# Folding three banks' maxima ahead of time in an attention loop on one core

## The chip, the core and the metric

The kernel runs on one core of a Trainium2 chip. Five engines matter: TensorE (PE in the profile; its weight loads are PEld), VectorE (DVE), ScalarE (ACT), GpSimd (POOL) and SyncE (SP), which issues the DMAs. Each engine works through its own queue in the order in which the program wrote it; semaphores tie the queues together. TensorE writes its results to PSUM, eight banks of 512 float32 columns in each of 128 partitions; everything else lives in SBUF or in HBM. The metric is the time of one execution in microseconds on the device; lower is better.

## What is computed

One layer of an encoder, for two sequences: a prompt of 512 rows and a sample of 2,048 rows, each 1,024 wide, all in float32. The input projection gives a pooled branch and an attention branch; after the output projection comes a gated feed-forward network with a convolution of width 3. The change touches attention alone:

```python
q_full = concatenate([q_nope, q_rope], -1)      # 8 heads, 64 + 32 wide
k_full = concatenate([k_nope, k_rope of all heads], -1)
s = einsum('bqhd,bkhd->bhqk', q_blk, k_full) * scale
p = softmax(s, axis=-1)
o = einsum('bhqk,bkhd->bqhd', p, v)             # v is 64 wide
```

Products are made from float16 halves: each operand is split into a high and a low part, and three of the four products are added up. That gives nearly float32.

## The kernel before

Attention is cut into 144 units. A unit is one head and one block of queries: 256 queries in the prompt (16 units, `nq` 2), 128 queries in the sample (128 units, `nq` 1). The scores of a unit lie transposed in PSUM: keys on the partitions, and in each bank four tiles of keys by 128 queries (in the prompt two tiles by 256). A sample unit has four banks, a prompt unit two. Seven of the eight PSUM banks rotate through the scores of successive units (`bank`, from psS and psT); the eighth, `x` (psX, `side_tile`), holds the small things of a unit side by side: the output of the products in its first 129 columns, and the transposed maxima in others.

A softmax needs, for each query, the maximum over all keys. With the scores transposed, the maximum runs over the partitions and over the tiles. The steps, with their letters in the written order and their lines, are these for unit `i`:

- scores of a bank on PE: twelve matmuls, L939 (L for bank 3 of unit i+1; a, b, c for banks 0, 1, 2 of unit i+2).
- maximum of a bank over its four tiles, on DVE: a reduction that reads PSUM, L951 (M for bank 3 of unit i+1; x, y, z for banks 0, 1, 2 of unit i+2). Bank `b` writes the adjacent 128 columns `mx4[:, b, :]`.
- fold (N, unit i+1): one DVE reduction over the four banks, L965. It reads `mx4` with its two last axes exchanged, so in steps of 128 values.
- T (unit i+1): the folded maxima are transposed on PE into `x`, L981, so that queries lie on partitions.
- d (unit i+1): DVE reduces them over the 128 columns (L989), which gives the maximum of each query, and splits it into two parts that add up exactly (L992, L995, four columns wide each).
- R (unit i+1): the parts are transposed back by PE (L1003), and ACT copies them out with the sign changed (mr, L1006).
- r (unit i): four small matmuls add the negative maximum to the four banks, L1015, at once in four row groups of the array.
- e0, e1 (unit i): ACT takes the exponential of a bank into `pf` in SBUF as float32, L1028. It frees the bank.
- h, f, i (unit i): the high half of `pf` in float16: bank 0 on ACT (L1042), bank 1 and then banks 2 and 3 together on DVE (L1040).
- l0 to l3 (unit i): the low half, one POOL subtraction for each bank, L1047.
- A, P (unit i-2): sixteen pairs of matmuls multiply the halves with the values, L1062 and L1063, ten pairs in A and six in P.
- o (unit i-2): ACT copies the output out of `x`, L1075, and after each fourth block POOL adds its halves, L1078. q: after each fourth block DVE divides by the sum, L1090 and L1096.

Between units a generator (`prep`) is advanced by one step in two units of four, from unit 36 on: it loads and scales the output projection's weights; 16 of its steps are a DVE reduction, L832.

The order within a unit is written by hand as a string, `ORDER` for units followed by a sample unit and `ORDER2` for the others; `START` has the first five. The framework keeps each engine's instructions in this order (`manual_schedule`) and adds semaphores for data and for buffers.

Of the kernel before, what the change touches and what calls it, by code (L numbers as in the profile page):

```python
# [11 lines left out]
F32 = mybir.dt.float32  # L12
F32R = mybir.dt.float32r
I32 = mybir.dt.int32
AF = mybir.ActivationFunctionType
ALU = mybir.AluOpType
AX = mybir.AxisListType
# [3 lines left out]
P = 128  # L21
# [27 lines left out]
def encoder(ctx, tc, ins, outs, seq_names=("x_prompt", "x_sample")):  # L49
    nc = tc.nc  # L50
    act, dve, pool, pe = nc.scalar, nc.vector, nc.gpsimd, nc.tensor
# [21 lines left out]
    ident = small([P, P], "ident")  # L73
# [140 lines left out]
    with tp("wA", 1) as wA, tp("pA", 2) as pA, tc.manual_schedule():  # L214
# [568 lines left out]
        k = NC - 1  # L783
# [109 lines left out]
    with tp("pB", 2) as pB, tp("psX", 1, "right", space=PSUM) as psX, \  # L893
# [9 lines left out]
        units = []  # L903
# [39 lines left out]
        def st_max(i, b):  # L943
            u = units[i]
            w = u["w"]
            t0, t1 = u["banks"][b]
            st = u["st"][b]
            if t1 - t0 == 4:
                if b == 0:
                    u["mx4"] = pB.tile([P, 4, P], F32, name=f"mx4_{i}", tag="mx4")  # L950
                dve.tensor_reduce(u["mx4"][:, b, :], st.rearrange("p (t q) -> p q t", q=w), axis=AX.X, op=ALU.max)  # L951
            elif b:
                for t in range(2):
                    dve.tensor_tensor(out=u["mx"][:, :w], in0=st[:, t * w:(t + 1) * w], in1=u["mx"][:, :w], op=ALU.max)
            else:
                u["mx"] = pB.tile([P, 256], F32, name=f"mx_{i}", tag="mx")
                dve.tensor_reduce(u["mx"][:, :w], st[:, :(t1 - t0) * w].rearrange("p (t q) -> p q t", q=w), axis=AX.X,
                                  op=ALU.max)

        def st_fold(i):  # L960

            u = units[i]
            if len(u["banks"]) == 4:
                u["mx"] = pB.tile([P, 256], F32, name=f"mx_{i}", tag="mx")
                dve.tensor_reduce(u["mx"][:, 0:P], u["mx4"].rearrange("p b q -> p q b"), axis=AX.X, op=ALU.max)  # L965

        def side_tile(i):

            if ("x", i) not in state:
                state["x", i] = psX.tile([P, 512], F32, name=f"x_{i}", tag="x")  # L970
            return state["x", i]

        def st_T(i):
            u = units[i]
            xp = side_tile(i - 1)
            old = units[i - 1 - LAG]["nq"] if i > LAG else 1
            u["alone"] = u["nq"] > 1 or old > 1
            u["mrp"] = xp[:, 512 - u["w"]:] if u["alone"] else xp[:, 129:129 + P]
            xp = u["xp"] = xp[:, 512 - u["w"]:]
            for j in range(u["nq"]):  # L980
                pe.matmul(xp[:, j * P:(j + 1) * P], u["mx"][:, j * P:(j + 1) * P], ident, is_transpose=True,  # L981
                          start=u["alone"], stop=True, skip_group_check=True)

        def st_redT(i):
            u = units[i]
            nq = u["nq"]
            mc = pB.tile([P, 2], F32, name=f"mc_{i}", tag="mc")
            m = mc[:, 0:nq]
            dve.tensor_reduce(m, u["xp"][:, :nq * P].rearrange("p (j k) -> p j k", j=nq), axis=AX.X, op=ALU.max)  # L989
            hi, lo = p3[:, 0:nq, :, 0], p3[:, 0:nq, :, 1]  # L990
            mb = m.rearrange("p (j o) -> p j o", o=1).to_broadcast([P, nq, 4])
            dve.tensor_scalar(out=hi.bitcast(I32), in0=mb.bitcast(I32), scalar1=-4096, scalar2=None,  # L992
                              op0=ALU.bitwise_and)
            for j in range(nq):
                dve.tensor_scalar(out=lo[:, j], in0=mb[:, j], scalar1=p3[:, j, 0, 0:1], scalar2=None,  # L995
                                  op0=ALU.subtract)

        def st_rep(i):

            u = units[i]  # L1000
            nq, w = u["nq"], u["w"]
            for j in range(nq):
                pe.matmul(u["mrp"][:, j * P:(j + 1) * P], p3[:, j].rearrange("p a b -> p (a b)"), ident,  # L1003
                          is_transpose=True, start=u["alone"], stop=True, skip_group_check=True)
            mr = pB.tile([P, 256], F32R, name=f"mr2_{i}", tag="mr2")
            act.activation(mr[:, :w], u["mrp"][:, :w], AF.Copy, scale=-1.0)  # L1006
            u["mr"] = mr

        def st_r1(i, b):
# [9 lines left out]
        def cols(u, b):  # L1019
            t0, t1 = u["banks"][b]  # L1020
            return slice(t0 * u["w"], t1 * u["w"])
# [9 lines left out]
        def st_hi(i, b):  # L1031
            u = units[i]
            if "ph" not in u:
                u["ph"] = pB.tile([P, 2048], F16, name=f"ph_{i}", tag="ph", bufs=3)
                u["pl"] = pB.tile([P, 2048], F16, name=f"pl_{i}", tag="pl", bufs=3)
            c = cols(u, b)
            if b == 2 and len(u["banks"]) == 4:
                c = slice(c.start, cols(u, 3).stop)
            if b in (1, 2):
                dve.tensor_copy(u["ph"][:, c], u["pf"][:, c])  # L1040
            elif b == 0:
                act.activation(u["ph"][:, c], u["pf"][:, c], AF.Copy)  # L1042

        def st_lo(i, b):
# [70 lines left out]
        def run(fn, k, *a):  # L1115
            if 0 <= k < NU:
                fn(k, *a)

        def some(fn, k, bs):
            if 0 <= k < NU:  # L1120
                for b in bs:
                    if b < len(units[k]["banks"]):
                        fn(k, b)
# [1 line left out]
        step = dict(  # L1125
            r=lambda i: some(st_r1, i, range(4)),
            e=lambda i: some(st_exp, i, range(4)),
            e0=lambda i: some(st_exp, i, range(3)),
            e1=lambda i: some(st_exp, i, [3]),
            A=lambda i: run(st_pv, i - LAG, 0),  # L1130
            P=lambda i: run(st_pv, i - LAG, 1),
            
            L=lambda i: some(st_scores, i + 1, [3]),
            a=lambda i: some(st_scores, i + 2, [0]),
            b=lambda i: some(st_scores, i + 2, [1]),
# [6 lines left out]
            x=lambda i: some(st_max, i + 2, [0]),  # L1142
            y=lambda i: some(st_max, i + 2, [1]),
            z=lambda i: some(st_max, i + 2, [2]),
            N=lambda i: run(st_fold, i + 1),
            f=lambda i: some(st_hi, i, [1]),
            h=lambda i: some(st_hi, i, [0]),
            i=lambda i: some(st_hi, i, [2]),
            l0=lambda i: some(st_lo, i, [0]),
            l1=lambda i: some(st_lo, i, [1]),  # L1150
            l2=lambda i: some(st_lo, i, [2]),
# [5 lines left out]
            q=lambda i: run(st_out2, i - LAG - 1))  # L1157
        START = ["a b x y", "a b T d t x u y R", "r e T d t R x y u f l1 h l0",
                 "r e T d t R x y u f l1 h l0", "r e T d A P R x y f l1 h l0 o q"]
        ORDER2 = "r e T d a b x R f l1 y h A P q o l0 c z"  # L1160
        ORDER = "r e0 A L M N P o e1 a T d f l1 b R i c h l0 l2 l3 x y z q"
        for i in range(-2, NU):
            whole = units[min(max(i, 0) + 1, NU - 1)]["nq"] == 1
            for x in (START[i + 2] if i + 2 < len(START) else ORDER if whole else ORDER2).split():
                step[x](i)
            if i >= NU // 4 and i % 4 in (0, 1):
                next(prep, None)
            if i == NU - 8:
                for _ in prep:
                    pass  # L1170
                c_load_m(0)
                c_load_m(1)
# [549 lines left out]
```

## Time and profile before

| | us |
|---|---|
| median of three runs (3251.7 to 3269.7) | 3259.68 |
| the profiled execution, its own time | 3256.74 |
| its span, from the first to the last instruction | 3254.9 |
| PE busy in the span | 3044.8 |
| DVE busy in the span | 2161.2 |
| attention stage, from the first add of maxima to the last exponential | 359 to 1272 |

The profile is one execution. "Busy" is the time in which an engine has an instruction under way; PE's matmuls overlap, so a busy PE can still be slower than at its peak. A table of waits says which engine stood idle, on which instruction, until what. A timeline lists instructions in order of time and merges those of one kind. The granted clock of TensorE is given as a share of 2.4 GHz; it has two levels, 1.2 and 2.4 GHz.

### The profile page before, as it was taken

The page shows a single profiled execution, that of the slowest core. Times are in us where ns is not written, and L with a number is a line of the kernel's source. Part 1 is how long each engine was busy: PE and PEld are TensorE (multiplying, and loading weights), DVE is VectorE, ACT ScalarE, POOL GpSimd, SP SyncE. Part 2 cuts the span into 40 slices and gives each one's busy share as a digit, 9 for nine tenths or more (in the row PEclk, how much of TensorE's full clock was granted, in tenths as well). Part 3 has the DMA queues.
Part 4 walks back from the last instruction along what each step waited for, and adds up shares of the span by engine and source line. Part 5 has one row for each costly group of instructions (what it writes and reads, how often), then busy time and mean ns, then how long its engine had stood idle before and what let it go on. Part 6 is the DMA issues. An engine that isn't in the chain of part 4 may idle for free. (4 is left out here: it accounts for less than half of the span.)

```text
span 3254.9 us, 59928 instructions
## 1 busy us (share of the span) xinstructions
PE 3044.8 (94%) x24601; PEld 1959.7 (60%) x24601; DVE 2161.2 (66%) x4783; ACT 1400.4 (43%) x2863; POOL 875.7 (27%) x825
## 2 busy tenths in 40 slices
PE   6999888888887888999999999999999999999998
PEld 4777577777776776444555555555545555555554
DVE  6677788788887887335777777734357666674333
ACT  4554556556565665223333333433333333333333
POOL 1211467777776775221000000000100000000000
PEclk9999899999998999999999999999999999999999
DMA  3333221201110102576111111311161111113112
GB/s 133 105 108 92 72 50 34 70 5 24 31 22 8 28 4 75 190 220 168 45 47 40 40 39 40 112 36 36 57 150 40 51 41 39 40 38 102 42 38 75
DMA packets 272061, 210.37 MB, mean 65 GB/s; under 512 B 48739, under 2 KB 247722, under 8 KB 271530
## 3 DMA queue, kind: packets, MB, share of 16 engines
q1 hardware_dynamic: 270012, 200.23, 21.1%
q0 software_dynamic: 1440, 5.24, 0.4%
q8 instruction: 193, 3.16, 0.4%
q10 hardware_dynamic: 334, 1.06, 0.1%
q14 instruction: 82, 0.67, 0.1%
HBM read 140.51 MB, written 55.38 MB: 60 GB/s over the span
## 5 line engine op out<-in xcount | busy, mean ns | idle before, releaser
L1288 PE MATMUL up<-h,ws 128*128 128x512 f16 (+1 forms) x6336 | 1146.6, 344 | 7.3 <-DMA h<-h_x_sample 5.9
L1288 PEld LDWEIGHTS <-ws 128*128 128x128 f16 x6336 | 619.9, 98 | 533.3 <-issue 6.1
L1047 POOL TENSOR_TENSOR pl<-pf,ph 128x512 f16<-128x512 f32 x544 | 660.6, 1242 | 239.9 <-DVE ph L1040 197.0
L1387 PE MATMUL dn<-G,wds 128*128 128x512 f16 (+1 forms) x3168 | 579.0, 344 | 0.0
L939 PE MATMUL st<-Q,K 96*128 96x128 f16 (+1 forms) x6336 | 469.4, 225 | 3.3 <-ACT pf L1028 2.1
L1387 PEld LDWEIGHTS <-wds 128*128 128x128 f16 x3168 | 310.0, 98 | 254.2
L939 PEld LDWEIGHTS <-K 96*128 96x128 f16 x6336 | 420.9, 102 | 14.7 <-issue 3.8
L1028 ACT ACTIVATE pf<-st,ln_shift,cs 128x512 f32<-128x512 f32 x544 | 392.7, 774 | 56.6 <-PE st L1015 47.0
L951 DVE TENSOR_REDUCE mx<-st 128x128 f32<-128x512 f32 x512 | 329.3, 684 | 70.3 <-PE st L939 69.5
L1293 ACT ACTIVATE c<-up,ctab 128x511 f32<-128x511 f32 (+3 forms) x264 | 182.1, 699 | 407.4 <-PE up L1288 401.0
L1294 DVE SCALAR_TENSOR_TENSOR c<-up,ctab,c 128x510 f32<-128x510 f32 (+3 forms) x264 | 173.5, 657 | 185.7 <-ACT c L1293 183.0
L1062 PE MATMUL x<-V,ph 128*128 128x129 f16 x2072 | 238.4, 232 | 0.4 <-ACT t L1075 0.4
L1063 PE MATMUL x<-V,pl 128*128 128x65 f16 x2072 | 228.9, 202 | 6.6 <-POOL pl L1047 6.6
L1062 PEld LDWEIGHTS <-ph 128*128 128x128 f16 x2176 | 211.3, 105 | 32.3 <-issue 32.2
L1063 PEld LDWEIGHTS <-pl 128*128 128x128 f16 x2176 | 207.2, 103 | 7.7 <-POOL pl L1047 7.3
L1394 DVE SCALAR_TENSOR_TENSOR yt<-dn,yscB,yt 128x512 f32<-128x512 f32 (+1 forms) x48 | 31.5, 660 | 227.5 <-ACT yt L1393 217.7
L1297 DVE SCALAR_TENSOR_TENSOR c<-up,ctab,c 128x511 f32<-128x511 f32 (+1 forms) x264 | 174.7, 662 | 9.3
L1006 ACT ACTIVATE mr<-x 128x128 fp32r<-128x128 f32 (+1 forms) x143 | 41.2, 288 | 276.0 <-PE x L1003 276.0
L130 ACT ACTIVATE ws<-wr,sF 128x1024 f16<-128x1024 f32 x88 | 96.2, 1138 | 147.0 <-DVE sF L1265 142.0
L1335 POOL PARTITION_ALL_REDUCE imrA<-imxA x2 | 0.7, 374 | 576.9 <-DVE imxA L1333 576.9
L1262 POOL PARTITION_ALL_REDUCE war<-wam x22 | 7.8, 356 | 527.0 <-DVE wam L1260 520.6
L1415 POOL TENSOR_TENSOR y<-y,fng 128x512 f32<-128x512 f32 (+1 forms) x42 | 45.3, 1083 | 384.4 <-ACT yp L1406 349.7
(410 smaller groups left out, 3716.4 us busy)
## 6 DMA issues: line engine op xcount, KB each, us to landing
wr<-in_w_up SPq DMA_DIRECT2D x88, 512.0 KB, 4.9
wd<-in_w_down SPq DMA_DIRECT2D x32, 512.0 KB, 4.3
x_s<-in_x_sample SPq DMA_DIRECT2D x8, 1024.0 KB
xt_Cs<-in_x_sample SPq DMA_DIRECT2D x8, 1024.0 KB, 7.8
x_x_sample<-xt_Cs SPq DMA_DIRECT2D x8, 1024.0 KB, 4.0
h_x_sample<-rows_Cs SPq DMA_DIRECT2D x16, 512.0 KB, 2.7
wd<-in_w_down SPq DMA_DIRECT2D x16, 384.0 KB, 3.5
y<-x_x_sample SPq DMA_DIRECT2D x3, 2048.0 KB, 8.7
```

The lines of the kernel that those rows point to most:

```text
L130: act.activation(hi, src, AF.Identity, scale=scale)
L939: pe.matmul(st[:, (t - t0) * w:(t - t0 + 1) * w], kt[:, x, t * P:(t + 1) * P], qt[:, y, u["q0"]:u["q0"] + w], start=n == 0 and t == t0, st ...
L951: dve.tensor_reduce(u["mx4"][:, b, :], st.rearrange("p (t q) -> p q t", q=w), axis=AX.X, op=ALU.max)
L1028: act.activation(u["pf"][:, c], u["st"][b][:, :c.stop - c.start], AF.Exp, bias=ln_shift[:, 0:1], scale=cs[:, 0:1])
L1047: pool.tensor_tensor(out=u["pl"][:, c], in0=u["pf"][:, c], in1=u["ph"][:, c], op=ALU.subtract)
L1062: pe.matmul(op[:, j, 0:129], u["ph"][:, c0:c0 + P], V[:, k0 + t, h, 0:129], start=t == 0, stop=False)
L1063: pe.matmul(op[:, j, 64:129], u["pl"][:, c0:c0 + P], V[:, k0 + t, h, 64:129], start=False, stop=t == nkt - 1)
L1288: pe.matmul(ps[:, :ncol], ws[side][:, k, x, :], ht[:, k, y, :ncol], start=m == 0, stop=m == 3 * KT - 1)
L1293: act.activation(c[:, :n], ps[:, :n], AF.Identity, scale=cw[:, 1, col:col + 1], bias=ctab[:, 3, col:col + 1])
L1294: dve.scalar_tensor_tensor(out=c[:, 1:n], in0=ps[:, 0:n - 1], scalar=cw[:, 0, col:col + 1], in1=c[:, 1:n], op0=ALU.mult, op1=ALU.add)
L1297: dve.scalar_tensor_tensor(out=c[:, 0:j1], in0=ps[:, 1:1 + j1], scalar=cw[:, 2, col:col + 1], in1=c[:, 0:j1], op0=ALU.mult, op1=ALU.add)
L1387: pe.matmul(acc[part][:, :n], w[f // 8][:, f % 8, x, :], G_[0][:, f, y, o:o + n], start=f in (0, NF - 1) and (x, y) == (0, 0), stop=f >= N ...
```

## The change

The maxima of banks 0 to 2 now go, one value in three, into `mx3` (128 queries by 3), and a fold (F, unit i+2) reduces these three right after the maximum of bank 2, at the end of the unit before. The maximum of bank 3 stays by itself in `mx2`. T transposes both, `mx` and `mx2`, side by side into 256 columns of `x`, and d reduces over all 256. Where the output of a prompt unit still needs those columns of `x` (three units), DVE takes the larger of the two first, and one transpose follows as before.

The transposes back (R) now write over the first columns of T's. All transposes start their group anew.

The high halves are cast in two parts: banks 0 and 1 by ACT (h), banks 2 and 3 by DVE (f).

The order within a sample unit: all four exponentials stand together; the scores a stand between A, L and P; M and x follow; the copy of the output, o, stands behind d, and the fold F and the cast f at the end. In a prompt unit the products A and P come first. A third string, `TURN`, serves the last prompt unit. The diff, without the unchanged lines between:

```diff
             if t1 - t0 == 4:
                 if b == 0:
-                    u["mx4"] = pB.tile([P, 4, P], F32, name=f"mx4_{i}", tag="mx4")
-                dve.tensor_reduce(u["mx4"][:, b, :], st.rearrange("p (t q) -> p q t", q=w), axis=AX.X, op=ALU.max)
+                    u["mx3"] = pB.tile([P, P, 3], F32, name=f"mx3_{i}", tag="mx3")
+                if b == 3:
+                    u["mx2"] = pB.tile([P, P], F32, name=f"mx2_{i}", tag="mx2")
+                dve.tensor_reduce(u["mx2"] if b == 3 else u["mx3"][:, :, b], st.rearrange("p (t q) -> p q t", q=w),
+                                  axis=AX.X, op=ALU.max)
...
-                dve.tensor_reduce(u["mx"][:, 0:P], u["mx4"].rearrange("p b q -> p q b"), axis=AX.X, op=ALU.max)
+                dve.tensor_reduce(u["mx"][:, 0:P], u["mx3"], axis=AX.X, op=ALU.max)
...
         def st_T(i):
             u = units[i]
-            xp = side_tile(i - 1)
-            old = units[i - 1 - LAG]["nq"] if i > LAG else 1
-            u["alone"] = u["nq"] > 1 or old > 1
-            u["mrp"] = xp[:, 512 - u["w"]:] if u["alone"] else xp[:, 129:129 + P]
-            xp = u["xp"] = xp[:, 512 - u["w"]:]
-            for j in range(u["nq"]):
-                pe.matmul(xp[:, j * P:(j + 1) * P], u["mx"][:, j * P:(j + 1) * P], ident, is_transpose=True,
-                          start=u["alone"], stop=True, skip_group_check=True)
+            parts = [u["mx"][:, j * P:(j + 1) * P] for j in range(u["nq"])]
+            if u["nq"] == 1:
+                if i > LAG and units[i - 1 - LAG]["nq"] > 1:
+                    dve.tensor_tensor(out=parts[0], in0=parts[0], in1=u["mx2"], op=ALU.max)
+                else:
+                    parts.append(u["mx2"])
+            xp = u["xp"] = side_tile(i - 1)[:, 512 - len(parts) * P:]
+            for j, part in enumerate(parts):
+                pe.matmul(xp[:, j * P:(j + 1) * P], part, ident, is_transpose=True, start=True, stop=True,
+                          skip_group_check=True)
...
-            dve.tensor_reduce(m, u["xp"][:, :nq * P].rearrange("p (j k) -> p j k", j=nq), axis=AX.X, op=ALU.max)
+            dve.tensor_reduce(m, u["xp"].rearrange("p (j k) -> p j k", j=nq), axis=AX.X, op=ALU.max)
...
-                pe.matmul(u["mrp"][:, j * P:(j + 1) * P], p3[:, j].rearrange("p a b -> p (a b)"), ident,
-                          is_transpose=True, start=u["alone"], stop=True, skip_group_check=True)
+                pe.matmul(u["xp"][:, j * P:(j + 1) * P], p3[:, j].rearrange("p a b -> p (a b)"), ident,
+                          is_transpose=True, start=True, stop=True, skip_group_check=True)
...
-            act.activation(mr[:, :w], u["mrp"][:, :w], AF.Copy, scale=-1.0)
+            act.activation(mr[:, :w], u["xp"][:, :w], AF.Copy, scale=-1.0)
...
             c = cols(u, b)
-            if b == 2 and len(u["banks"]) == 4:
-                c = slice(c.start, cols(u, 3).stop)
-            if b in (1, 2):
+            if len(u["banks"]) == 4:
+                c = slice(c.start, cols(u, b + 1).stop)
+            if b:
                 dve.tensor_copy(u["ph"][:, c], u["pf"][:, c])
-            elif b == 0:
+            else:
                 act.activation(u["ph"][:, c], u["pf"][:, c], AF.Copy)
...
-            N=lambda i: run(st_fold, i + 1),
-            f=lambda i: some(st_hi, i, [1]),
-            h=lambda i: some(st_hi, i, [0]),
-            i=lambda i: some(st_hi, i, [2]),
+            F=lambda i: run(st_fold, i + 2),
+            h=lambda i: run(st_hi, i, 0),
+            f=lambda i: run(st_hi, i, len(units[i]["banks"]) // 2) if i >= 0 else None,
...
-        ORDER2 = "r e T d a b x R f l1 y h A P q o l0 c z"
-        ORDER = "r e0 A L M N P o e1 a T d f l1 b R i c h l0 l2 l3 x y z q"
+        ORDER2 = "r e A P o T d a b x R f l1 y h q l0 c z F"
+        TURN = "r e A L a P M x T d o b h f R y l0 l1 c z F q"
+        ORDER = "r e A L a P M x T d o b h R y l0 l1 c z F f l2 l3 q"
...
-            whole = units[min(max(i, 0) + 1, NU - 1)]["nq"] == 1
-            for x in (START[i + 2] if i + 2 < len(START) else ORDER if whole else ORDER2).split():
+            now, then = (units[min(max(k, 0), NU - 1)]["nq"] for k in (i, i + 1))
+            order = START[i + 2] if i + 2 < len(START) else ORDER if now == 1 else TURN if then == 1 else ORDER2
+            for x in order.split():
                 step[x](i)
```

## Rows read from the trace of the kernel before

**Rows 1.** Page: busy us (share of the span), instructions of each engine.

```profile
PE 3044.8 (94%) x24601; PEld 1959.7 (60%) x24601; DVE 2161.2 (66%) x4783; ACT 1400.4 (43%) x2863; POOL 875.7 (27%) x825
```

**Rows 2.** Stretch: us, busy us of PE, PEld, DVE, ACT, POOL; clock, DMA, GB/s.

```profile
440.00:1240.00 800.00, 678.27 (x10434) 590.36 (x10432) 660.50 (x1320) 471.48 (x859) 612.76 (x519) 0.95 0.11 26
```

**Rows 3.** Waits, 440 to 1240 us: us in total, times, longest us.

```profile
PE x L981 <- DVE mx L965: 89.8, 118, 1.6
```

**Rows 4.** Timeline of one unit: start us, us, engine, line, operation [idle before <-releaser].

```profile
678.16 0.50 PE L1015 MATMUL st<-mr,ones 2*128 2x512 f32 x4
...
678.75 2.12 ACT L1028 ACTIVATE pf<-st,ln_shift,cs 128x512 f32<-128x512 f32 x3 [0.36 <-PE st L1015]
...
679.58 0.83 PE L939 MATMUL st<-Q,K 96*128 96x128 f16 x12
...
680.25 0.22 PE L1062 MATMUL x<-V,ph 128*128 128x129 f16 x1
...
680.45 0.69 DVE L951 TENSOR_REDUCE mx<-st 128x128 f32<-128x512 f32 x1
...
680.77 0.83 PE L939 MATMUL st<-Q,K 96*128 96x128 f16 x12
...
681.17 1.06 DVE L965 TENSOR_REDUCE mx<-mx 128x128 f32<-128x512 f32 x1
...
682.38 0.30 PE L981 MATMUL x<-ident,mx 128*128 128x128 f32 x1 [0.78 <-DVE mx L965]
...
682.72 0.29 DVE L989 TENSOR_REDUCE mc<-x 128x1 f32<-128x128 f32 x1 [0.48 <-PE x L981]
...
683.54 0.33 PE L1003 MATMUL x<-ident,p 128*128 128x128 f32 x1 [0.19 <-DVE p L995]
...
684.47 0.51 PE L1015 MATMUL st<-mr,ones 2*128 2x512 f32 x4
```

**Rows 5.** Groups by shape (busy us, mean ns), three stretches; then a timeline row.

```profile
L989 DVE TENSOR_REDUCE mc<-x 128x2 f32<-128x256 f32 x15 | 6.3, 421 | 9.6 <-PE x L981 9.6
...
L832 DVE TENSOR_REDUCE am<-w_o 128x1 f32<-128x512 f32 x16 | 10.8, 676 | 0.0
...
L1040 DVE CAST ph<-pf 128x1024 f16<-128x1024 f32 x121 | 83.0, 686 | 0.0
...
L1488 ACT ACTIVATE rows_Cs<-xn_Cs 128x1024 f16<-128x1024 f32 x16 | 16.9, 1057 | 26.6 <-DVE xn_Cs L1485 25.5
...
400.60 0.41 PE L981 MATMUL x<-ident,mx 128*128 128x128 f32 x2 [0.35 <-DVE ri L1090]
```

**Rows 6.** Lines L995, L1096: ns min/median/max; timeline at 421 us of POOL and DVE.

```profile
L995 DVE TENSOR_SCALAR p<-mc,p x160: 219/231/1072, 357.5 to 1267.2; 128x4 f32<-128x4 f32 x160
...
L1096 DVE TENSOR_TENSOR o<-t,ri x40: 425/439/1111, 381.5 to 1284.1; 128x256 f32<-128x256 f32 x40
...
421.24 0.73 POOL L1078 TENSOR_TENSOR t<-t 128x256 f32<-128x256 f32 x1
421.93 1.15 POOL L1047 TENSOR_TENSOR pl<-pf,ph 128x512 f16<-128x512 f32 x1
...
422.04 1.20 DVE L995 TENSOR_SCALAR p<-mc,p 128x4 f32<-128x4 f32 x2
```

**Rows 7.** Timeline at 126 us: two reads by ACT and one by DVE.

```profile
126.22 0.47 ACT L130 ACTIVATE lT_s<-tl_s,gs 128x256 f16<-128x256 f32 x1
...
126.58 0.36 ACT L128 ACTIVATE krT_s<-tl_s 32x256 f16<-32x256 f32 x1
...
126.97 0.48 DVE L135 SCALAR_TENSOR_TENSOR lT_s<-tl_s,gs,lT_s 128x256 f16<-128x256 f32 x1 [2.11 <-ACT krT_s L128]
```

**Rows 8.** Two copies of R (timeline), and the stretch 691.00 to 694.40 between them.

```profile
690.22 0.28 ACT L1006 ACTIVATE mr<-x 128x128 fp32r<-128x128 f32 x1 [1.99 <-PE x L1003]
...
697.84 0.28 ACT L1006 ACTIVATE mr<-x 128x128 fp32r<-128x128 f32 x1 [1.84 <-PE x L1003]
...
691.00:694.40 3.40, 3.40 (x39) 3.15 (x36) 1.54 (x4) 2.13 (x4) 3.40 (x4) 0.52 0.00 0
```

More of the change, by code (lines that the diff above doesn't have):

```diff
@@ L1127, in encoder @@
             e=lambda i: some(st_exp, i, range(4)),
-            e0=lambda i: some(st_exp, i, range(3)),
-            e1=lambda i: some(st_exp, i, [3]),
             A=lambda i: run(st_pv, i - LAG, 0),
```

## The prediction

> **What bounds the kernel now.** I read the busy line of the page first: PE is busy for 94% of the span [rows 1], so a gain must come from where PE still waits. The table by stretch finds that place: from 440 to 1240 us, inside the attention loop, PE is busy for 678 of 800 us, DVE for 661, POOL for 613 and ACT for 471, at a granted clock of 0.95 [rows 2]. No engine is full there, so a chain of waits sets the pace. The table of waits names it: PE's first transpose (L981) waits for DVE's fold of the maxima (L965) 118 times, 89.8 us in all [rows 3].
>
> The timeline of one unit gives the chain [rows 4]. I set zero at the add of the row maxima (L1015, 678.16): first exponential 0.59, scores of the fourth bank (L) 1.42, their maximum (M) 2.29, fold 3.01, transpose (T) 4.22, second reduction (d) 4.56, transposed split maximum (R) 5.38, next add 6.31. The maximum, the fold of 1.06 and the way to the transpose are its middle. PE stands 0.78 us before T and 0.19 before R. The unit is 6.31 us long, and 128 such units run.
>
> **What the change moves, with nothing in its way.** The fold goes to the end of the unit before. T then needs only M, and PE now has the scores of the next first bank (a) and the end of the products (P) to do before it. L takes 0.67 of PE and P 0.52 [rows 4]: a at 1.42+0.67 = 2.09 (the second exponential frees its bank: three take 2.12, so it ends at 0.59+0.67+0.77 = 2.03), P at 2.76, T at 3.28. M is over at 2.29+0.69 = 2.98, so PE itself is last there. Two transposes take 0.41 [rows 5]: to 3.69, d at 3.73. d reads 256 columns, 0.42 instead of 0.29 [rows 5]: to 4.15. From d's end to R it is 0.53 now (682.72+0.29 to 683.54): R at 4.68, and 0.93 later, as now, the next add: 5.61. PE would wait only about 0.5 us before R.
>
> ACT must keep up. Its copy of the output (o) stands behind d in program order, and reads the PSUM bank that d reads. [Rows 7] show what that does elsewhere. ACT reads one half of a bank until 126.69 and the other until 126.94. DVE, idle for 2.11 us, needs the first half and ACT's first result alone, but starts at 126.97, 0.03 us after the second read. So I let o wait for d. o 4.19 to 4.47 (0.28, like the copy of the same size in [rows 8]); then the cast of two banks (h), 1.06 [rows 5] against 0.62, to 5.43; then the copy of R, to 5.61; add at about 5.65. That is 0.66 less than 6.31: 84 us in 128 units. The casts on DVE become one of 0.69 [rows 5]. The fold reads 384 adjacent values: between 0.54 (the adjacent 512 of [rows 5] take 0.68; a quarter off the part that is streamed) and 0.80 (three quarters of 1.06). I take 0.54; the cast behind it waits for something else, as follows, and either hides.
>
> **What stands in its way: POOL and DVE exclude each other.** In [rows 6] DVE's tensor_scalar L995 (four columns, median 0.23) takes up to 1.07 us: it starts at 422.04, while a POOL subtraction (L1047) runs from 421.93, and ends 0.03 after it. L1096, median 0.44, goes up to 1.11. In the full loop these rows stay at their medians, because POOL's pause (it is busy for 613 of 800 us, 4.8 of a unit's 6.31) lies where DVE does its small steps. By those alone the price is nothing and the sum is 84 us less.
> The Trainium skill, SBUF — State Buffer, section Who interferes with whom, says that the port pair which DVE's copies, casts, tensor_scalars and two-input operations share with GpSimd goes to whoever issues first, for the whole instruction. By it the price is what follows, and [rows 6] agree.
> I take the meetings as real and lay out POOL, with 1.15 for each of four subtractions [rows 6]. The first two need h: 5.5 to 7.8. DVE's cast needs the maximum of bank three (scores from about 4.85, read from 5.71 to 6.40) and the fold (to 6.94); it finds POOL busy until 7.8, and ends 0.6 later, at 8.4. The other two subtractions need the cast: 8.45 to 10.75. In the next unit, with one unit D long, d ends at D+4.15, and the two small steps behind it wait until 10.75. R comes 0.36 after that (0.03, L995 and two hand-overs), the add 0.93 later: 12.04. So two units take at least 12.04 together, 6.02 each, not 5.65: of 0.66 less than half is left.
> Two things come every fourth unit. The output's normalization (L1090, L1096) is behind the cast on DVE and asks 0.3 after its end; the third subtraction started 0.05 after it. So L1096 waits until 9.6 and ends at about 9.9, and M of the next unit, queued behind it, starts 9.9-(5.75+2.29) = 1.86 late. M has 0.2 to spare against P; T and all behind it, o and h too, come 1.66 later: a unit of 5.65+1.66 = 7.31. POOL's chain from h starts that much later too, so the next add comes at 12.04+1.66 = 13.70: a unit of 6.39. And the output's add on POOL (L1078, 0.72 [rows 6]) now comes right behind the fourth subtraction and holds DVE's L995 until its end: L995, else at D+4.35, waits some 0.64, a unit of 6.29, and one of 12.04-6.29 = 5.75 follows. Four units: 7.31+6.39+6.29+5.75 = 25.74, 6.43 each, 0.12 more than 6.31.
>
> **The sum.** 128 x 0.12 = +15 us. The preparation of the output weights puts 16 reductions of 0.68 [rows 5] behind the cast in other units, now hidden; M has 0.2 to spare, and the rest is partly taken by the wait on POOL: +0.25 each, +4. In the first stage (16 units of the short sequence) the products go ahead of the transposes: a later T by 8 pairs of 0.09 (P has six in 0.52), in turn PE no longer has to do them after R. Between -4 (0.3 in 13 units) and +9 (0.7 in each); I take 0, as PE fills either gap. The clock: 17 of the full units show 7.48 to 7.62 us between two copies of R instead of 6.31, such as that of [rows 8], where the granted clock was 0.52 of full for 3.4 us, so at its lower level, 1.2 GHz; 22 us together. PE's idle stretch before T or R is at times longer than now: between -22 (none is left) and +22 (twice as many); I take a quarter more, +6, since [rows 2] says how small the share is now. Together +25. The profiled execution took 3256.74 us (span 3254.9), the median of the three runs is 2.9 above it: 3256.74+25+2.9 = 3285.
>
> **Rivals.** A: o does not wait for d, because they read other columns. POOL's chain starts 0.46 earlier, so two units take 11.58; L1096 ends at 9.44, M is 1.5 and T 1.3 late: 6.95, then 12.88-6.95 = 5.93; the unit of the output's add is 0.5 longer, 6.15, the fourth 5.65. Four units take 24.68, 6.17 each: 128 x 0.14 = 18 us less, with the preparation's 4 and no loss to the clock 3246. For it speaks that nothing but the bank is shared; against it [rows 7]. B: the two engines don't meet, as in the full loop now: 84 us less, 3176, with fewer stretches at half clock perhaps 3165. Against it stands that POOL's last two subtractions now start later, and so end among DVE's small steps. C: they meet, but the normalization and the output's add fall into a pause more often than I lay out: with half their cost over 24.08, four units take 24.9, 6.23 each, 10 us less; with the other terms 3260, no change. For it: one shift of 0.3 us decides whether DVE or POOL asks first. Against it: the third subtraction is released by the cast itself, and so is always just ahead. D: the three maxima, which now store every third word, become slow. If each took 0.38 more (the fold that reads in steps takes 1.06, the adjacent reduction 0.68 [rows 4, 5]), the one between M and d would put d 0.3 later in every unit: 38 us more than my sum, 3323. Only that difference of rows speaks for it, and these stores come once in four reads.
> The Trainium skill, SBUF — State Buffer, section Door 1: The DMA port swizzle, says that accesses which cross to another 16-byte line each pay a penalty. By it a store every 12 bytes would pay too; no run here shows a stepped store of that length.
>
> **How the numbers follow.** My forecast 0.48, A 0.14, B 0.10, C 0.23, D 0.05. My forecast's own range is 3263 to 3307, plus and minus the clock's 22. About 16 us, 0.5%, is what a measurement can tell from no change. Slower by more than that: most of the forecast (0.42), D and some of C (0.05), 0.52. Within it: the rest of the forecast, most of C and half of A, 0.31. Faster: B and the other half of A, 0.17. The range from 3230 to 3314 takes in A and C; B, D and the ends are left out.
>
> **What would show it.** In the changed profile: PE's wait before T gone in three of four units (right for the first step); L992 or L995 with a mean well over 0.17 and 0.23, the 1,024-wide cast over 0.69, and L1096 at about 1.4 in the full loop (right for the port); ACT's copy of the output starting 0.04 after d's end (right for the bank; if it starts after the transposes, A holds); the time between two copies of R in a pattern of four, with one near 7.3. A flat 5.65 would speak for B, maxima well over 0.70 for D. A median under 3260 makes my forecast wrong.

## The result, and the profile after

The changed kernel takes 3290.35 us (median of 12 runs, 3263.5 to 3299.5) against 3253.66 for the kernel before on the same chips: a ratio of 1.0103, 95% interval 1.0080 to 1.0126. It is slower by about 37 us, where 25 had been forecast (3285, in a range of 3263 to 3307). The profiled execution of it took 3288.59 us, with a span of 3286.8; before it was 3256.74 and 3254.9.

The new lines are shifted: the maxima are L953, the fold L968, the transposes L987, d L995, its two small steps L998 and L1001, the transposed split maximum R L1009 and its copy L1012, the add L1021, the cast on DVE L1046 and on ACT L1048, the subtractions L1053, the output's copy o L1081, its add on POOL L1084, the normalization L1096 and L1102.

First the busy line of the page, and below it the stretch from 440 to 1240 us (columns as in [rows 2]):

```profile
PE 3076.3 (94%) x24726; PEld 2000.3 (61%) x24726; DVE 2183.2 (66%) x4658; ACT 1446.1 (44%) x2863; POOL 842.5 (26%) x825
```

```profile
440.00:1240.00 800.00, 682.07 (x10092) 606.17 (x10092) 651.58 (x1151) 491.73 (x820) 554.34 (x495) 0.91 0.10 23
```

The mean granted clock is 0.91 instead of 0.95 [rows 2]; PE is as busy as it was in these 800 us (682 against 678), DVE and POOL are less, though fewer units now fit in. So the loop still waits, in other places. The waits of that stretch (us in total, times, longest us):

```profile
ACT t L1081 <- DVE mc L995: 192.0, 116, 3.4
...
PE x L1009 <- DVE p L1001: 48.2, 88, 1.5
...
PE x L987 <- DVE mx L953: 31.4, 40, 1.3
```

The 118 waits of T for the fold [rows 3] are gone, as meant; 40 of T for the maximum M are left. In their place PE waits ahead of R for DVE's small steps, and o waits for d in every unit. What those steps cost stands in the groups by shape (busy us, mean ns), against [rows 5, 6]:

```profile
L1053 POOL TENSOR_TENSOR pl<-pf,ph 128x512 f16<-128x512 f32 x465 | 534.5, 1170 | 229.4 <-issue 131.5 <-ACT pf L1034 29.1 <-DVE ph L1046 25.9
...
L953 DVE TENSOR_REDUCE mx<-st 128x128 f32<-128x512 f32 x465 | 312.2, 685 | 123.2 <-PE st L939 123.0
...
L1046 DVE CAST ph<-pf 128x1024 f16<-128x1024 f32 x116 | 131.9, 1137 | 0.0
...
L968 DVE TENSOR_REDUCE mx<-mx 128x128 f32<-128x384 f32 x116 | 64.1, 553 | 3.9
...
L995 DVE TENSOR_REDUCE mc<-x 128x1 f32<-128x256 f32 x115 | 47.5, 413 | 9.8 <-PE x L987 7.6
L998 DVE TENSOR_SCALAR p<-mc 128x4 int32<-128x4 int32 x116 | 42.1, 363 | 4.0
L1102 DVE TENSOR_TENSOR o<-t,ri 128x256 f32<-128x256 f32 x29 | 37.7, 1301 | 2.8
...
L1001 DVE TENSOR_SCALAR p<-mc,p 128x4 f32<-128x4 f32 x116 | 30.6, 264 | 4.1
```

The cast has a mean of 1.14 us instead of 0.69, L998 0.36 instead of 0.17, the normalization 1.30 instead of 0.44; the reductions L953 and L995, between and beside the same subtractions, keep their length (0.69 and 0.41). The fold takes 0.55 (0.54 had been taken).

The timeline of one unit of every four, the long one, from the add at 806.56, with the add ahead of it (columns as in [rows 4]):

```profile
800.24 0.51 PE L1021 MATMUL st<-mr,ones 2*128 2x512 f32 x4
...
805.98 2.27 POOL L1053 TENSOR_TENSOR pl<-pf,ph 128x512 f16<-128x512 f32 x2 [0.76 <-POOL pl L1053]
806.00 0.28 ACT L1012 ACTIVATE mr<-x 128x128 fp32r<-128x128 f32 x1
806.56 0.51 PE L1021 MATMUL st<-mr,ones 2*128 2x512 f32 x4
...
807.87 0.94 DVE L1046 CAST ph<-pf 128x1024 f16<-128x1024 f32 x1
...
808.88 2.45 POOL L1053 TENSOR_TENSOR pl<-pf,ph 128x512 f16<-128x512 f32 x2 [0.63 <-DVE ri L1096]
809.00 1.32 DVE L1102 TENSOR_TENSOR o<-t,ri 128x256 f32<-128x256 f32 x1
...
809.85 0.30 PE L987 MATMUL x<-ident,mx 128*128 128x128 f32 x1
...
810.25 1.28 DVE L953 TENSOR_REDUCE mx<-st 128x128 f32<-128x512 f32 x2
...
810.98 0.33 PE L987 MATMUL x<-ident,mx 128*128 128x128 f32 x1 [0.83 <-DVE mx L953]
...
811.44 0.41 DVE L995 TENSOR_REDUCE mc<-x 128x1 f32<-128x256 f32 x1
...
811.88 0.28 ACT L1081 ACTIVATE t<-x 128x129 f32<-128x129 f32 x1 [1.94 <-DVE mc L995]
812.06 1.05 ACT L1048 ACTIVATE ph<-pf 128x1024 f16<-128x1024 f32 x1
...
813.01 0.27 ACT L1012 ACTIVATE mr<-x 128x128 fp32r<-128x128 f32 x1
```

The cast asks behind the fold and ends 0.56 after the second subtraction (808.25); the third subtraction, 1.16 long, is then 0.12 ahead of L1102, which ends at 810.32, 0.28 after it; M stands behind it. Of T's two transposes the one of the fold comes at 3.29 of the unit (3.28 by the forecast), the one that needs M at 4.42. The next three copies of R come at 819.20, 825.09 and 831.43: units of 7.01, 6.19, 5.89 and 6.34 us.

Over the 127 units between the 17th and the 144th copy of R, 31 hold more than 0.8 us at half clock (1.2 instead of 2.4 GHz), with a mean of 8.20 us; the other 96 have a mean of 6.445. Before these are 21 units of 7.98 and 106 of 6.317. So of the profiled execution's 31.9 us more, 127 x 0.128 = 16 stand in the units at full clock, and 31 x 1.76 - 21 x 1.66 = 20 in those with half clock; the 15 steps of the first stage, from the first to the 16th copy, take 2 less (63.1 instead of 65.3), and what lies ahead and behind 2 less.

### The profile page after: what moved, and what is told of

The parts are those of the page before. It is cut to its first block, busy times and chain, and to the rows that moved or that the text cites. A ratio compares the mean times of both kernels' runs of the same rounds, so it can differ in the third digit from the quotient of the medians.

```text
span 3286.8 us, 60149 instructions
## 1 busy us (share of the span) xinstructions
PE 3076.3 (94%) x24726; PEld 2000.3 (61%) x24726; DVE 2183.2 (66%) x4658; ACT 1446.1 (44%) x2863; POOL 842.5 (26%) x825
## 3 DMA queue, kind: packets, MB, share of 16 engines
q10 hardware_dynamic: 334, 1.06, 0.1%
## 5 line engine op out<-in xcount | busy, mean ns | idle before, releaser
L1053 POOL TENSOR_TENSOR pl<-pf,ph 128x512 f16<-128x512 f32 x544 | 626.4, 1172 | 293.5 <-issue 140.4
L939 PEld LDWEIGHTS <-K 96*128 96x128 f16 x6336 | 438.1, 105 | 14.5 <-issue 4.0
L953 DVE TENSOR_REDUCE mx<-st 128x128 f32<-128x512 f32 x512 | 343.9, 685 | 132.5 <-PE st L939 132.2
L1034 ACT ACTIVATE pf<-st,ln_shift,cs 128x512 f32<-128x512 f32 x544 | 379.8, 777 | 116.6 <-PE st L1021 104.1
L1046 DVE CAST ph<-pf 128x1024 f16<-128x1024 f32 (+1 forms) x144 | 151.8, 1054 | 2.6 <-ACT pf L1034 2.6
L135 DVE SCALAR_TENSOR_TENSOR wds<-wd,fs,wds 128x128 f16<-128x128 f32 x352 | 114.0, 381 | 50.4 <-ACT wds L130 50.4
L1048 ACT ACTIVATE ph<-pf 128x1024 f16<-128x1024 f32 (+1 forms) x144 | 144.1, 1001 | 0.0
```

What stands on the lines that cost most here:

```text
L939: pe.matmul(st[:, (t - t0) * w:(t - t0 + 1) * w], kt[:, x, t * P:(t + 1) * P], qt[:, y, u["q0"]:u["q0"] + w], start=n == 0 and t == t0, st ...
L953: dve.tensor_reduce(u["mx2"] if b == 3 else u["mx3"][:, :, b], st.rearrange("p (t q) -> p q t", q=w), axis=AX.X, op=ALU.max)
L1034: act.activation(u["pf"][:, c], u["st"][b][:, :c.stop - c.start], AF.Exp, bias=ln_shift[:, 0:1], scale=cs[:, 0:1])
L1053: pool.tensor_tensor(out=u["pl"][:, c], in0=u["pf"][:, c], in1=u["ph"][:, c], op=ALU.subtract)
```

## The experiments

Seven kernels ran. The interval is that of the ratio to the kernel before on the same chip, which took 3250.0 us beside e1 to e4 and 3254.8 beside e5 to e8; the row "before" is that of the result. A unit with half clock is one that holds more than 0.8 us of it.

| run | us | ratio to before, 95% | mean unit at full clock | units with half clock |
|---|---|---|---|---|
| before | 3253.66 | 1 | 6.32 | 21 of 127 |
| after | 3290.35 | 1.0080 to 1.0126 | 6.44 | 31 |
| e1_cast_early | 3163.4 | 0.9714 to 0.9747 | 5.76 | 4 |
| e2_norm_ahead | 3265.9 | 1.0033 to 1.0066 | 6.31 | 26 |
| e3_fold_alone | 3204.5 | 0.984 to 0.988 | 6.06 | 6 |
| e4_pe_filled | 3240.4 | 0.9963 to 0.9985 | 6.37 | 2 |
| e5_before_filled | 3229.9 | 0.9908 to 0.9943 | 6.33 | 1 |
| e7_out_ahead_of_d | 3205.5 | 0.9831 to 0.9871 | 6.06 | 5 |
| e8_half_subtractions | 3220.2 | 0.9877 to 0.9916 | 6.15 | 11 |

**The cast at another place.** To be told apart: do POOL and DVE hold each other up, or does ACT's chain (o behind d, then the cast of two banks) set the pace?

```
-ORDER = "r e A L a P M x T d o b h R y l0 l1 c z F f l2 l3 q"
+ORDER = "r e A L a P M x T d f o b h R y l2 l3 c z F l0 l1 q"
```

> The changed kernel with one edit: DVE's cast of banks two and three (f) stands right behind the second reduction (d), and POOL takes the subtractions of these banks first, then those of banks zero and one. No work is added or left out, and ACT's copy of the output (o) still waits for d. Theory (the loss is POOL and DVE excluding each other at d's small steps, the cast and the normalization): the cast runs from 4.56 to 5.25 of the unit, while POOL rests; POOL goes 5.3 to 9.9; d of the next unit ends at 5.65+4.15 = 9.8, so its two small steps lose 0.1 at most; the normalization meets a subtraction, but M has time to spare. The output's add still costs about 0.6 every fourth unit. 5.65 to 5.85 per unit instead of 6.44 at full clock, 75 to 100 us less: about 3200, with L1046 near 0.69 and L998 near 0.18 in the mean. Rival (the wait of o for d, and the cast of two banks behind it on ACT, set the pace): these stand as before, the unit stays at 6.4 and the time at 3290.

Measured: 3163.4 us, 127 less than the change by the medians (121 by the ratios to the kernel before) and faster than both kernels. The units at full clock follow each other as 5.68, 5.68, 5.75, 5.88. The groups of 440 to 1140 us:

```profile
L1048 ACT ACTIVATE ph<-pf 128x1024 f16<-128x1024 f32 x120 | 125.8, 1048 | 0.0
L1046 DVE CAST ph<-pf 128x1024 f16<-128x1024 f32 x120 | 82.4, 687 | 0.2 <-issue 0.2
...
L998 DVE TENSOR_SCALAR p<-mc 128x4 int32<-128x4 int32 x120 | 29.0, 242 | 4.1
...
L1102 DVE TENSOR_TENSOR o<-t,ri 128x256 f32<-128x256 f32 x30 | 18.2, 608 | 2.9
```

The work is the same, instruction for instruction; only the cast and the two pairs of subtractions stand elsewhere. The cast is back at 0.69, L998 at 0.24 (0.18 expected), and ACT's cast, untouched at 1.05, does not set the pace at 6.4. The rival falls. The gain is larger than the 75 to 100 expected: the half-clock units went from 31 to 4 as well.

**The normalization at another place.**

```
-ORDER = "... c z F f l2 l3 q"
+ORDER = "... c z F q f l2 l3"
```

> The changed kernel with the output's normalization (q) moved ahead of DVE's cast f, behind the fold. Theory (every fourth unit is 7.26 us long because L1102 asks 0.1 after the third subtraction has started, and M stands behind it): it now asks at about 7.1, while the second subtraction runs to 7.8, and M is late no more. The unit of 7.26 goes; the cast starts 0.3 later in that unit, and what POOL does behind it too. A cycle of four takes 24.4 to 25.2 instead of 25.65, 15 to 40 us less: 3250 to 3275, with fewer stretches at half clock nearer the lower end; L1102 has a mean of 0.6 to 1.0. Rival (the 7.26 has another cause, such as the store of the output to memory in the same unit): the pattern stays 6.18, 5.88, 6.33, 7.26, 3290.

Measured: 3265.9. The cycle is 6.52, 5.88, 6.60, 5.88 = 24.9 us (24.4 to 25.2 expected), the unit of 7.26 is gone, and L1102 has a mean of 0.73:

```profile
L1102 DVE TENSOR_TENSOR o<-t,ri 128x256 f32<-128x256 f32 x26 | 19.0, 732 | 2.9 <-DVE ri L1096 0.5
```

The store to memory moved together with it, so this edit alone does not part the two. But only every second head stores, and in the changed kernel with PE's waits filled (e4, below) a unit of 7.00 to 7.26 comes in every cycle of every head; so the rival falls. 24 us less by the medians (18 by the ratios to the kernel before), of which 127 x 0.137 = 17 are in the units at full clock.

**The fold alone.** In the kernel before, the maxima go to the new tiles, the fold of three banks to the end of the order, and T makes two transposes, with R over their first columns; the casts stay.

```
-ORDER = "r e0 A L M N P o e1 a T d f l1 b R i c h l0 l2 l3 x y z q"
+ORDER = "r e0 A L M P o e1 a T d f l1 b R i c h l0 l2 l3 x y z F q"
```

> The kernel before with the fold of three banks ahead of time and the two transposes alone: the order of before, the fold put at the end, its casts as before (bank zero on ACT, bank one on DVE right behind d, banks two and three on DVE in front of the scores). Theory (the fold ahead is the gain, the merged and later cast is the loss): T at 3.3 instead of 4.22, less 0.13 for the wider d, the chain would be 5.6; but DVE's second cast now asks right when POOL's first subtraction runs (5.0 to 6.2), and DVE then has three maxima and the fold, 2.6, in front of the next M: 9.3 instead of 7.9. 5.7 to 6.2 per unit: 3190 to 3245, so faster than before. Rival (the fold ahead brings nothing, since PE or ACT take its place): 3250 to 3260, the unit at 6.3.

Measured: 3204.5, faster by 46 us than the kernel before on the same chip (3250.0), at 6.06 per unit (5.7 to 6.2 expected). So the fold ahead of time is a gain; the order and the merged cast that came with it turned 46 us less into 37 more. Here POOL is the one held up: its subtraction has a mean of 1.24 us, and 1.17 in the changed kernel. The kernel before has the same 1.24; first its group and two rows of its timeline, then two groups of this run:

```profile
L1047 POOL TENSOR_TENSOR pl<-pf,ph 128x512 f16<-128x512 f32 x424 | 515.4, 1244 | 159.3 <-DVE ph L1040 125.5 <-PE x L1003 25.0 <-issue 7.0
```

```profile
683.39 1.02 DVE L1040 CAST ph<-pf 128x512 f16<-128x512 f32 x2
...
683.95 1.47 POOL L1047 TENSOR_TENSOR pl<-pf,ph 128x512 f16<-128x512 f32 x1 [1.48 <-DVE ph L1040]
```

```profile
L1053 POOL TENSOR_TENSOR pl<-pf,ph 128x512 f16<-128x512 f32 x450 | 547.7, 1244 | 129.5 <-DVE ph L1046 99.8 <-PE x L1009 20.3 <-issue 6.8
...
L1046 DVE CAST ph<-pf 128x1024 f16<-128x1024 f32 x112 | 76.7, 685 | 0.0
```

In that row the subtraction starts while the second cast runs, and ends 1.01 after the cast's end (684.41). One in four does so in both kernels, with a median of 1.47 us; most of the others take 1.15.

**PE's waits filled, after and before.** These two take the clock out of the comparison. In both a function, `filler`, writes n matmuls into a score bank ahead of the scores that overwrite it, in units of four banks alone.

```
+            n = 8 if b == 1 else 20 if b == 0 and (u["q0"] // P) % 4 == 1 else 0
+            filler(i, b, n)
...
+            for k in range(n):
+                pe.matmul(st[:, 0:w], kt[:, 0, 0:P], qt[:, 0, u["q0"]:u["q0"] + w], start=k == 0, stop=True,
+                          skip_group_check=True)
```

That is the changed kernel; in the kernel before the same function is called by one line:

```
+            filler(i, b, 10 if b == 0 else 0)
```

> The changed kernel with matmuls added where PE waits, into the same score banks and overwritten there by the scores behind them: 8 of 128 columns (0.45 us) ahead of the scores of each second bank, in PE's wait before R, and 20 more (1.1 us) ahead of those of the first bank in each fourth unit, the one with the late M. Nothing else is changed. Theory on the clock (31 of 127 full units hold a stretch at half clock, 55 us in all against 35 before, and PE's idle time before T and R is what lets the granted clock fall): few such stretches are left, under 12 units, and the time falls by 15 to 40 us in spite of the added work: 3250 to 3275. Rival (the clock falls for another reason, or the added work is on the path): as many such stretches as now, and 3290 or more.

> The kernel before with ten matmuls of 128 columns (0.56 us) added in each full unit, ahead of the scores of the next first bank (a) and into its bank, where the scores overwrite them: in PE's wait of 0.78 us before T. Theory on the clock (PE's wait before T lets the granted clock fall in the kernel before too, 21 of 127 full units, 35 us): at most 6 such units are left, and the time falls by 20 to 30 us: 3220 to 3232. Between the changed kernel filled in the same way (3240) and this one there then stands only the unit at full clock and the preparation, 15+4 = 19 us by the prediction, less the 2 of the first stage: 10 to 20. Rival (the clock falls whatever PE does, and the changed kernel gained from its filling in another way): 21 such units, 3250 or more.

Measured: after 3240.4, before 3229.9. More work on PE made the changed kernel 50 us faster by the medians (42 by the ratios to the kernel before), more than the 15 to 40 expected, and the kernel before 25 us faster, as expected. The stretch from 440 to 1240 us, after and then before:

```profile
440.00:1240.00 800.00, 750.80 (x12343) 677.26 (x12341) 699.69 (x1224) 525.40 (x874) 591.22 (x526) 0.99 0.11 27
```

```profile
440.00:1240.00 800.00, 739.86 (x11970) 649.08 (x11968) 678.69 (x1357) 484.48 (x881) 628.72 (x532) 0.99 0.11 27
```

The granted clock goes from 0.91 and 0.95 to 0.99 in both; 2 units and 1 with half clock are left, among them the one near 1000 us which every kernel has. So the fall of the clock followed PE's waits. Its price in the change is 50 - 25 = 25 us more than before by the medians, 46 - 27 = 19 by the profiled executions and 42 - 24 = 18 by the ratios to the kernel before on the same chip. The changed kernel in this state goes 7.00, 6.18, 5.88, 6.18 = 25.24 per cycle (25.65 with two of the preparation's reductions in it), the one before 4 x 6.32 = 25.28. At full clock the units of the two kernels are as fast as each other.

**The output's copy ahead of d**, in the kernel with the early cast:

```
-ORDER = "r e A L a P M x T d f o b h R y l2 l3 c z F l0 l1 q"
+ORDER = "r e A L a P M x T o d f b h R y l2 l3 c z F l0 l1 q"
```

> The kernel with DVE's early cast (3163 us), with one edit: ACT's copy of the output (o) stands between the transposes and the second reduction d, not behind d; both read the same bank. Theory (two readers of one bank follow each other in the order of the program, whichever engine they are on): now d waits for o. o goes 3.73 to 4.01, d 4.05 to 4.47 instead of 3.73 to 4.15, R and the next add 0.32 later; the cast on ACT, 0.46 earlier, no longer sets the end. The unit goes from 5.75 to 5.9 to 6.1: 3180 to 3205. Rival (o follows d for another reason, so in this order both read at once): d stays where it is, ACT is 0.46 earlier and frees the copy of R: 3150 to 3165.

Measured: 3205.5, 42 more than with o behind d (39 by the ratios to the kernel before; half a microsecond above the range expected), at 5.99 per unit and 6.23 in the one with the output's add. One unit's three rows:

```profile
739.65 0.41 PE L987 MATMUL x<-ident,mx 128*128 128x128 f32 x2
...
740.11 0.28 ACT L1081 ACTIVATE t<-x 128x129 f32<-128x129 f32 x1 [0.35 <-PE x L987]
...
740.42 0.42 DVE L995 TENSOR_REDUCE mc<-x 128x1 f32<-128x256 f32 x1 [0.39 <-ACT t L1081]
```

Now DVE's d starts 0.03 after ACT's read of the same bank has ended, with T done 0.36 before. The two read different columns. What orders them is a wait that the program has between two engines that use the same tile, `x`, in its own order. The tile is the whole bank, so no run here tells the tile from the bank.

**Half of two subtractions.** The change's own order; POOL's third and fourth subtractions cover 256 of 512 columns, and the products of the columns left out take the high part for the low one, so the output lacks that part.

```
             c = cols(u, b)
+            if b > 1:
+                c = slice(c.start, c.start + 256)
             pool.tensor_tensor(out=u["pl"][:, c], in0=u["pf"][:, c], in1=u["ph"][:, c], op=ALU.subtract)
...
-                pe.matmul(op[:, j, 64:129], u["pl"][:, c0:c0 + P], V[:, k0 + t, h, 64:129], start=False,
+                pe.matmul(op[:, j, 64:129], u["ph" if t > 7 and t % 4 > 1 else "pl"][:, c0:c0 + P], V[:, k0 + t, h, 64:129], start=False,
```

> The changed kernel in its own order; POOL's third and fourth subtractions cover half of their columns, 256 instead of 512, and the products of the columns left out take the high part for the low one: this leaves work out on POOL, and nothing on the other engines. Theory (what holds DVE up is the time for which POOL runs): the third and fourth now take some 0.6 each and end at 9.65, ahead of the next d's small steps; the normalization waits 0.5 instead of 0.9, so M is some 1.3 late in each fourth unit, a unit of 6.8 to 7.0, and the others go to 5.65 to 5.9. 5.9 to 6.1 per unit instead of 6.44, and fewer stretches at half clock: 3205 to 3250. Rival (DVE's small steps and casts are long for a reason of their own, such as ACT's cast of two banks beside them): the cast stays at 1.14, L998 at 0.36, and the time at 3290.

Measured: 3220.2; the units are 6.77 in each fourth and 5.74 else, until the preparation's reductions come (5.9 to 6.3 then); the mean of 6.15 is a little above the range expected. 440 to 1140 us:

```profile
L1046 DVE CAST ph<-pf 128x1024 f16<-128x1024 f32 x110 | 151.2, 1374 | 0.0
L1055 POOL TENSOR_TENSOR pl<-pf,ph 128x256 f16<-128x256 f32 x220 | 149.3, 700 | 67.9 <-ACT pf L1034 32.0 <-DVE ph L1046 18.9 <-DVE ri L1098 15.7
...
L1104 DVE TENSOR_TENSOR o<-t,ri 128x256 f32<-128x256 f32 x28 | 23.3, 833 | 2.7
L998 DVE TENSOR_SCALAR p<-mc 128x4 int32<-128x4 int32 x110 | 18.9, 172 | 3.8
```

Less work on POOL alone gives L998 back its 0.17 and takes the normalization from 1.30 to 0.83, against 0.44 before. The cast got longer, 1.37: it asks earlier, and still ends 0.55 after the second subtraction, which was left whole. The rival would have left L998, the cast and the time as they were, so it falls.

## Why the prediction was right, and where its terms were not

**T needs only M: right.** T comes right behind P in the units without a late M (waits for M 40 times in 116 units, those with the late M and those thrown out of step), and the fold alone is worth 46 us.

**o waits for d: right.** o starts 0.03 after d's end in all 116 units from 440 to 1240 us, and e7 shows the same order turned round. Rival A (3246) falls.

**POOL and DVE exclude each other: right**, and the point on which the sign hung. By the forecast two units take at least 12.04; 6.18 + 5.88 = 12.06 was measured. The cast was to end at 8.4 after the add of the unit before; by the timeline it ends at 808.81 - 800.24 = 8.57. L1102 was to end at about 9.9: 810.32 - 800.24 = 10.08. Take most of the meetings away and the unit falls to 5.68 (e1), next to the 5.65 that stood without them; rival B's number was right, its condition was not.
One premise was wrong, the one that B rests on: that the two do not meet in the full loop of the kernel before. DVE's rows keep their medians there, but a quarter of POOL's subtractions take 1.47 instead of 1.15 behind DVE's cast (683.95 above). There POOL is the one that waits, where it has time; the new order turned the waiting round, onto DVE, which M and R need.
The Trainium skill, SBUF — State Buffer, section Who interferes with whom, also says that on trn2 tensor_reduce never contends with GpSimd. The groups agree: the maxima have a mean of 685 ns and d 413 amid the subtractions that stretch the casts and small steps.

**The maxima's stepped stores: 685 ns** against 0.69 before, so rival D falls.
The Trainium skill's rule on accesses to another 16-byte line (SBUF — State Buffer, section Door 1: The DMA port swizzle), weighed for it, makes no difference that these stores show.

**The output's add holds L995: wrong, the step that failed in the cycle.** It was to keep the second small step waiting and so make a unit of 6.29 and one of 5.75 out of two of 6.02. The timeline of such a unit:

```profile
823.97 0.23 DVE L998 TENSOR_SCALAR p<-mc 128x4 int32<-128x4 int32 x1
823.97 0.28 ACT L1081 ACTIVATE t<-x 128x129 f32<-128x129 f32 x1 [0.83 <-DVE mc L995]
...
824.23 0.23 DVE L1001 TENSOR_SCALAR p<-mc,p 128x4 f32<-128x4 f32 x1
824.33 0.73 POOL L1084 TENSOR_TENSOR t<-t 128x256 f32<-128x256 f32 x1 [0.16 <-ACT t L1081]
```

The add needs o, and o starts with L998: at o's end, 824.25, L1001 has already begun, and the add comes 0.10 behind it. Nothing waits for it here. From 440 to 1240 us this is so for 20 of 29 adds, and for 27 of 31 in the filled kernel (e4), whose cycle is used below; in the other 9 and 4 the add comes first and L1001 takes 0.65 to 0.67 us, as forecast. So the unit ahead of the normalization is 6.18 and not 5.75 long, 0.43 of the wait for POOL is over before M is asked for, and the late unit with its follower takes 7.00 + 6.18 = 13.18 instead of 13.70. The cycle is 25.24, not 25.74, and at full clock the term of the units is 0, not +15. Rival C had named this add; its cycle of 24.9 took half of the cost off, and 0.50 of 1.66 came off.

**The preparation: right.** Two reductions in a cycle make it 25.65 instead of 25.24, 0.2 each, +3 for the 16 (+4 taken).

**The clock: too small, the step that failed in the sum.** I had taken a quarter more half-clock time, +6, out of a range of -22 to +22. It went from 82 to 154 us of half clock between the 17th and 144th copies; by the filled kernels the price is +18 to +25. I had written that PE's idle stretches would at times be longer, and still priced them by the clock's share in the stage before. That share could not tell: between the same copies PE is idle for 128 us before and 130 after, counted in pieces of over 0.15 us, but 5 pieces before and 62 after are over 0.9 us. That the longer pieces are what made the clock fall is not shown: e7 has 32 such pieces and only 5 units with half clock. Of the 31 units with half clock, 13 come right behind the unit with the late M and 6 at each of the other three places of the cycle. A half-clock unit also throws POOL and DVE out of the cycle (6.6 or 7.25 where 5.88 and 6.18 would come): of the 16 us that the units at full clock take more, the filled kernels leave 4, (6.365 - 6.333) x 127, with the preparation in them.

**The first stage**: -2 in the profiled execution, taken as 0. The six kernels that run it in the new order take 61.9 to 67.5 us for its 15 steps, with 10 to 24 us at half clock, so -2 is not told from nothing.

Together 0 + 3 and 18 to 25 for the clock are 21 to 28, against a forecast of 25, and 37 measured by medians, 32 in the profiled executions. That the sum came out near is luck: one term was 15 too high and another 12 to 19 too low. The filled kernels differ by 10.5 us in their medians, and the terms without the clock give 3 of them. In their profiled executions (13 us) 6 stand in the loop and 6 ahead of it, where neither is filled; there, from the first to the 17th copy, the changed kernel has 23.9 us at half clock and the one before 13.7. What is left beyond the terms, some 10 us, is not settled.

## What to carry to other kernels

Shortening the chain that ends last pays only as far as the second engine of a pair that cannot run at once still finds its pause: lay out both engines over two units, and put the long copy or cast into the pause, not behind the next producer (here one cast put elsewhere, with the subtractions that it releases, was worth about 125 us). Where TensorE waits in pieces of about a microsecond, price its clock first: matmuls of no use, put into the wait, show in one run how much of a change is clock (here 42 to 50 of 3290 us and 25 of 3255). An estimate of a rare step should ask which of two engines asks first, by name and by tenths of a microsecond; that is where this one went wrong.

## What the runs showed that had not been expected

- Added work that is thrown away makes both kernels faster: 8 more matmuls in each unit and 20 more in each fourth bring 42 to 50 us, 10 in each unit of the kernel before 25 us.
- Who asks first holds the other to the end of its instruction, in both directions: DVE's cast of 0.69 took 1.37 us in the mean behind a subtraction (e8), and POOL's subtraction of 1.15 took 1.47 behind DVE's cast (e3, and the kernel before). What is held has a rest to do after the other's end: 0.03 us for the small steps, 0.28 for the normalization, 0.55 for the cast, 1.01 for the subtraction.
- A three-word step in the store of a reduction cost nothing (685 ns), while the fold that read with steps had taken 1.06 for 512 values and takes 0.55 for 384 adjacent ones.
